# Two more gate blocks as a pair by seven products, and the constants of linear attention built earlier

## The chip, the cores and the metric

The kernel runs on one core of a Trainium2 chip. The metric is the device time in microseconds of one launch, from the first instruction to the last; a profile of one execution gives the time of every instruction on each engine: TensorE (PE, with its weight loads PEld), VectorE (DVE), ScalarE (ACT), GpSimd (POOL), and SyncE (SP), whose queue issues most transfers (DMA).

## What is computed

One layer of a streaming encoder over T = 1056 tokens (1024 of a prompt, 32 of a sample), width 1024:

```python
h = rms(x); z = h @ w_in   # GLA q,k,v,r,rank | band q,k,v | merge gates ga, gb
oa, s_gla = gla_branch(qa, ka, va, ra, alr, ...)      # 4 heads, causal gated linear recurrence
ob, k_rows, v_rows = attn_fn(qb, kb, vb, rel_bias)     # 8 heads, 64-frame chunks, band of 8 chunks back
mix = (sigmoid(ga) * (oa @ w_br_a) + sigmoid(gb) * (ob @ w_br_b)) @ w_out
x = x + rms_norm(mix, g_post_mix)
f, conv_new = conv_ffn(rms_norm(x, g_pre_ffn), conv_s0, w_up, conv_w, conv_b, w_down)
x = x + rms_norm(f, g_post_ffn)
x = x + rms_norm(sigmoid(rms_norm(x, g_pre_ple) @ w_ple_gate) * (pe @ w_ple), g_post_ple)
```

The gates `ga` and `gb` are 1024 columns of `w_in` each, so 8 blocks of 128 columns each. The outputs are y for both groups, the newest band rows, the states of linear attention (`o_gp` of the prompt, `o_gs` of the sample) and of the convolution.

## The kernel before

Tokens lie along the free axis, features on the 128 partitions. Every large product is made of three matmuls in fp32r: a value is split into a high part and the rest (`whi`, `wlo` of weights, `xh`, `xl` of the input), and high x high, high x low and low x high are summed in PSUM. A high part is made by ACT, a low part by DVE or POOL. One block of 128 weight columns over all tokens (`project`) is 8 feature tiles x 3 spans of 352 tokens x 3 = 72 matmuls of 352 columns; a third of it, one span, is 24.

The program runs: the norm of x (its sums `accx` and the result `rstd` are DVE's), four pairs of band heads (`band_project`, scores `s`, sums `sm`), four heads of linear attention (GLA), the gates, the merge, `w_out`, and the ConvFFN, whose large products `two` take seven products of half blocks.

A GLA head (`gla_head`) takes 8 chunks of 128 prompt tokens and the sample as the ninth. Per chunk PE transposes (`kt`), makes scores level by level, DVE copies them under the `masks` (`copy_predicated`), and PE multiplies scores by `vt` (L977) and state by queries (L979); DVE updates `state` (L989, three buffers). The sample's state is loaded into such a buffer (L970). `out_o_gp` and `out_o_gs` are stored by SP when the last states are there. A norm of the outputs `ot` follows (ACT square L997, DVE L999, split L259 and L260, matmuls L262 and L263, ACT, DVE). The masks (7 levels), `eye` and zeroed score tiles are built once by `constants`, with 28 affine selects on POOL and 8 casts on DVE, when GLA starts.

Gate blocks are made in two ways. Plain: `gates` calls `project`. By seven products: `gate_pair` takes two blocks of weights and halves of tokens and features and makes seven products of 4 feature tiles x 2 spans of 264 tokens x 3 = 24 matmuls each (`b11`, `b21`, `b22`, `t4`, `t2`, `t1`, `t3`), 168 in all. Three of them, and `t4` over the input's own quarter, need sums of quarters of x: these are made in the band (`quarter_sums`, tiles `tt`), stored to `d_t` in DRAM, and loaded again in eight transfers (`quarter_load`, L1039) and split (L1043 on ACT, L1044 on DVE) when `take` asks for them. Before the change the blocks 2 to 7 of `ga` are plain; the other two of `ga` and the eight of `gb` make five pairs.

Program order is not issue order: a scheduler sorts the instructions of every engine by data, buffers and priority, and the plain gates, written after the last head, fill PE between that head's small matmuls. Each engine and each queue then runs its rows strictly in that order. Pools bound what can move: `gp` (GLA's tiles) has to be released before `tp` and `gs` (tiles of the pairs) can be allocated, and `sums_left` (transfers that add up quarters of `w_down`) is drained first. `third_sum` (L1612) forms one input of the ConvFFN's `t3` by a subtraction of 128 x 1056 on POOL, twice.

Of the kernel before, what the change touches and what calls it, by code (L numbers as in the profile page):

```python
# [12 lines left out]
F32R = mybir.dt.float32r  # L13
# [4 lines left out]
P = 128  # L18
# [44 lines left out]
PLAIN_GATES = (2, 3, 4, 5, 6, 7)  # L63
# [58 lines left out]
def emit(tc, a):  # L122
# [365 lines left out]

    d_ob = tl(dram, [4, P, T], tag="d_ob")
# [198 lines left out]
    def quarter_sums(k):  # L688
        a1, a2, b1, b2 = [[t[:, r].bitcast(F32) for t in (xh, xl)] for r in (k, k + HK) for _ in range(2)]
        n = HT // QN  # L690
        for j in range(QN):
            p, q = slice(j * n, (j + 1) * n), slice(HT + j * n, HT + (j + 1) * n)
            A, S = ALU.add, ALU.subtract
            t = tl(bp, [P, n], tag="tt", bufs=12)
# [4 lines left out]
            t = tl(bp, [P, n], tag="tt", bufs=12)  # L699
# [4 lines left out]
            u = tl(bp, [P, n], tag="tt", bufs=12)  # L704
# [3 lines left out]
            t = tl(bp, [P, n], tag="tt", bufs=12)  # L708
# [4 lines left out]
    for hp in range(4):  # L713
# [34 lines left out]
        if hp:  # L748
            band_norm(hp - 1)
    bp.release()  # L750
# [15 lines left out]
    masks, eye, scores, scores_s = None, None, [], None  # L766


    def constants():
        nonlocal masks, eye, scores_s  # L770
        masks = tl(gp, [P, 7, P], U8, tag="masks")
        scores.extend(tl(gp, [P, 2 * P], tag=f"scores{i}") for i in range(2))
        for l in range(7):
            m = 1 << l
            mf = scores[l % 2][:, :P]
            po.memset(mf, 1.0)
            for j in range(2):
                v = blocks(mf, m)[:, :, m * j : m * j + m]
                first = m * (1 - j)
                pat = [[-2 * m, 64 // m], [0, m]]  # L780
                po.affine_select(out=v, in_=v, pattern=pat, compare_op=ALU.is_ge, fill=0.0, base=-first, channel_multiplier=1)
                pat = [[2 * m, 64 // m], [0, m]]
                po.affine_select(out=v, in_=v, pattern=pat, compare_op=ALU.is_ge, fill=0.0, base=first + m - 1, channel_multiplier=-1)
            ve.tensor_copy(masks[:, l], mf)
        eye = tl(gp, [P, P], U8, tag="eye")
        ve.tensor_copy(eye, ident)
        for i in range(2):
            po.memset(scores[i], 0.0)
        scores_s = tl(gp, [NS, NS], tag="scores_s")
        po.memset(scores_s, 0.0)  # L790

    DG = (192, 0)
    TOGETHER = ((4,3,2,1),(6,5))
    SEGS = [(0, 256), (256, 256), (512, 256), (768, 288)]

    def blocks(t, m):
        return t.rearrange("p (n s) -> p n s", s=2 * m)

    def apart(t, m):
        return bass.AP(t.tensor, t.offset, [t.ap[0], [2 * m, 64 // m], [P + m, 2], [1, m]])  # L800

# [1775 lines left out]
```

## Time and profile before

| | |
|---|---|
| median of 3 runs | 1895.81 us (1894.96 to 1901.61) |
| profiled execution | 1895.03 us, its span 1893.3 us |
| PE busy | 1866.0 us, 99% |
| DVE busy | 1347.5 us, 71% |
| ACT busy | 905.2 us, 48% |
| POOL busy | 434.0 us, 23% |

The span runs from the first to the last instruction of the profiled execution; busy times are those of instructions that compute, and matmuls that overlap count once. All stretches and start times below are microseconds from the span's start.

### The profile page before, as it was taken

What the parts mean: (1) busy time and instruction counts of PE and PEld (TensorE: products, weight loads), DVE (VectorE), ACT (ScalarE), POOL (GpSimd) and SP (SyncE); (2) the same over time, 40 slices, a digit from 0 to 9 for tenths busy, and PEclk for the clock granted to TensorE, in tenths of its full rate; (3) what the DMA queues carried; (4) which work ended last, traced back from release to release, by engine and by line L of the source; (5) the groups of instructions that cost most, each with busy time, mean ns of one, the idle gap of its engine ahead of it and who ended that gap; (6) DMA issues with size and microseconds to landing.
All of it is one profiled execution on the core that took longest, in us unless ns stands there. A gap on an engine that the chain in (4) does not pass through costs nothing.

```text
span 1893.3 us, 34755 instructions
## 1 busy us (share of the span) xinstructions
PE 1866.0 (99%) x13484; PEld 1836.2 (97%) x13484; DVE 1347.5 (71%) x2713; ACT 905.2 (48%) x1709; POOL 434.0 (23%) x548
## 2 busy tenths in 40 slices
PE   9999999999999999999999999999999999999997
PEld 8999999989999999999999999999999999999997
DVE  6657577678787774887463887987777776556886
ACT  7455465445454564544234564433333345445554
POOL 2312232342212121003210212332222222115312
PEclk9999999999999999999999999999999999999999
DMA  7324356452423433695484446543433448656677
GB/s 277 122 98 151 114 156 161 136 147 68 111 68 109 124 114 112 232 356 218 123 333 146 145 152 225 189 167 127 149 133 121 148 161 293 193 182 205 209 265 149
DMA packets 112417, 316.46 MB, mean 167 GB/s; under 512 B 14004, under 2 KB 39036, under 8 KB 112124
## 3 DMA queue, kind: packets, MB, share of 16 engines
q1 hardware_dynamic: 86124, 226.30, 35.5%
q0 software_dynamic: 25296, 87.04, 15.9%
q8 instruction: 106, 1.74, 0.4%
q10 hardware_dynamic: 832, 0.90, 0.1%
q14 instruction: 59, 0.48, 0.1%
HBM read 222.12 MB, written 111.93 MB: 176 GB/s over the span
## 4 chain that ended last, share of the span: by engine, by line
PE 84%; DVE 7%; issue 3%; ACT 3%; DMA 1%; POOL 0%; SPq 0%; ACTq 0%; DVEq 0%; POOLq 0%
PE mm L240 12%; PE mm L241 12%; PE mm L242 12%; PE c L2003 11%; PE two L1739 6%; PE two L1741 6%; PE two L1740 6%; PE aux L2003 2%; PE mm L1089 2%; PE mm L1091 2%; PE mm L1090 2%; PE one L615 2%; PE one L573 2%; PE two L919 1%; PE two L557 1%
## 5 line engine op out<-in xcount | busy, mean ns | idle before, releaser
L240 PE MATMUL mm<-xh,whi 128*128 128x352 f32 (+2 forms) x1008 | 333.5, 331 | 1.7 <-DVE q L813 1.1
L242 PE MATMUL mm<-xh,wlo 128*128 128x352 f32 (+2 forms) x1008 | 331.5, 329 | 0.0
L241 PE MATMUL mm<-xl,whi 128*128 128x352 f32 (+2 forms) x1008 | 330.3, 328 | 0.0
L220 POOL TENSOR_TENSOR wlo<-raw,whi 128x512 fp32r<-128x512 f32 x108 | 155.9, 1450 | 657.6 <-ACT whi L219 628.0
L240 PEld LDWEIGHTS mm<-xh,whi 128*128 128x128 f32 x1008 | 190.1, 189 | 3.9 <-DVE q L813 1.4
L242 PEld LDWEIGHTS mm<-xh,wlo 128*128 128x128 f32 x1008 | 189.4, 188 | 1.9 <-issue 1.0
L241 PEld LDWEIGHTS mm<-xl,whi 128*128 128x128 f32 x1008 | 189.9, 188 | 1.0
L1741 PE MATMUL two<-mh,wlo 128*128 128x264 f32 x576 | 162.9, 284 | 0.0
L1740 PE MATMUL two<-ml,whi 128*128 128x264 f32 x576 | 162.5, 283 | 0.0
L1739 PE MATMUL two<-mh,whi 128*128 128x264 f32 x576 | 161.3, 284 | 0.4 <-ACT whi L245 0.4
L219 ACT ACTIVATE whi<-raw 128x512 fp32r<-128x512 f32 x116 | 72.5, 628 | 119.4 <-PE mm L241 72.3
L2003 PE MATMUL c<-mh,whi 128*128 128x264 f32 x396 | 112.4, 284 | 0.0
L2003 PE MATMUL c<-mh,wlo 128*128 128x264 f32 x396 | 112.2, 283 | 0.0
L2003 PE MATMUL c<-ml,whi 128*128 128x264 f32 x396 | 112.2, 283 | 0.0
L1740 PEld LDWEIGHTS two<-ml,whi 128*128 128x128 f32 x576 | 108.3, 188 | 0.0
L1741 PEld LDWEIGHTS two<-mh,wlo 128*128 128x128 f32 x576 | 108.3, 188 | 0.0
L1739 PEld LDWEIGHTS two<-mh,whi 128*128 128x128 f32 x576 | 107.3, 188 | 0.6 <-ACT whi L245 0.6
L1729 ACT ACTIVATE whi<-ws 128x512 fp32r<-128x512 f32 x72 | 45.3, 629 | 89.0 <-PE two L1740 52.2
L566 ACT ACTIVATE s<-s,sm 128x640 f32<-128x640 f32 (+5 forms) x72 | 50.3, 698 | 58.5 <-DVE sm L564 57.2
L240 PE MATMUL mm<-mh,ahi 128*128 128x352 f32 x240 | 77.4, 322 | 0.0
L241 PE MATMUL mm<-ml,ahi 128*128 128x352 f32 x240 | 77.4, 322 | 0.0
L242 PE MATMUL mm<-mh,alo 128*128 128x352 f32 x240 | 77.3, 322 | 0.0
(649 smaller groups left out, 5929.1 us busy)
## 6 DMA issues: line engine op xcount, KB each, us to landing
raw<-in_w_in SPq DMA_DIRECT2D x51, 512.0 KB, 3.9
uraw<-d_b POOLq DMA_DIRECT2D x33, 528.0 KB, 4.9
raw<-in_w_up SPq DMA_DIRECT2D x26, 512.0 KB, 3.7
d_b<-av POOLq DMA_DIRECT2D x44, 264.0 KB, 2.7
d_s<-in_w_down POOLq DMA_DIRECT2D x16, 704.0 KB, 8.0
draw<-d_s SPq DMA_DIRECT2D x16, 704.0 KB, 4.2
hn<-d_b POOLq DMA_DIRECT2D x40, 264.0 KB, 3.8
d_b<-hn POOLq DMA_DIRECT2D x40, 264.0 KB, 2.5
```

Source lines behind the costliest of these rows:

```text
L219: ac.activation(hi[-1][:, d], raw[:, b], AF.Copy)
L220: eng.tensor_tensor(lo[-1][:, d], raw[:, b], hi[-1][:, d], op=ALU.subtract)
L240: pe.matmul(ps, h, xh(kt), start=(first and i == 0), stop=False)
L241: pe.matmul(ps, h, xl(kt), start=False, stop=False)
L242: pe.matmul(ps, l, xh(kt), start=False, stop=(last and i == n - 1))
L566: ac.activation(s, s, AF.Exp, scale=-1.0, bias=sm[:nq], accum_out=sums[:nq, q0 // P : q0 // P + 1])
L573: pe.transpose(tp[:n, i * nq : (i + 1) * nq], s[:, k0 : k0 + n], ident[:nq, :nq])
L1729: ac.activation(h, x, AF.Copy)
L1739: pe.matmul(ps[:, j, :HC], w[0][:, k], x[0][:, k, s], start=st, stop=False, skip_group_check=True)
L1740: pe.matmul(ps[:, j, :HC], w[0][:, k], x[1][:, k, s], start=False, stop=False, skip_group_check=True)
L1741: pe.matmul(ps[:, j, :HC], w[1][:, k], x[0][:, k, s], start=False, stop=sp_, skip_group_check=True)
L2003: pe.matmul(ps, w, x, start=st, stop=sp_, skip_group_check=True)
```

## The change

- Blocks 2 and 3 of `ga` leave the plain gates and become a sixth pair by seven products.
- The first two products of the first pair, `b11` and now `b21` (it was `b22`), are written ahead of the drain of `sums_left`, of the release of `gp` and of the pools `tp` and `gs`. What the first `take` calls loaded and split in steps over three products is asked for at the third.
- `constants` moves from GLA's start into the band loop, at the second pair of band heads with low priority, with a pool `cp` of its own that is released with `gp`.
- `tt` has 8 buffers in place of 12, and `third_sum` runs on DVE.

```diff
-PLAIN_GATES = (2, 3, 4, 5, 6, 7)
+BEFORE = 2
+PLAIN_GATES = (4, 5, 6, 7)
...
+    cp = pool("cp")
...
-            t = tl(bp, [P, n], tag="tt", bufs=12)
+            t = tl(bp, [P, n], tag="tt", bufs=8)
...
+        if hp == 1:
+            with low(QLOW):
+                constants()
...
-    constants()
     got = gla_project(0)
...
     gates(len(PLAIN_GATES))
-    for _ in sums_left:
-        pass
-    gp.release()
...
             (lambda: weight("b11", a11), m_b11),
+            (lambda: weight("b21", a12), m_b21),
             (for_b22, m_b22),
-            (lambda: weight("b21", a12), m_b21),
...
-    todo = [(w + n, lambda i, g, d=d, n=n: gate_done(d, n + i, g)) for w, d, ns in ((GB0, d_gb, (0, 2, 4, 6)), (GA0, d_ga, (0,))) for n in ns]
+    todo = [(w + n, lambda i, g, d=d, n=n: gate_done(d, n + i, g)) for w, d, ns in ((GB0, d_gb, (0, 2, 4, 6)), (GA0, d_ga, (0, 2))) for n in ns]
...
+    unit(0)[0]()
+    unit(1)[0]()
+    for i in range(BEFORE):
+        unit(i + LOOK)[0]()
+        unit(i)[1]()
+    for _ in sums_left:
+        pass
+    gp.release()
+    cp.release()
...
-    unit(0)[0]()
-    unit(1)[0]()
-    for i in range(7 * len(todo)):
+    for i in range(BEFORE, 7 * len(todo)):
         if unit(i + LOOK):
             unit(i + LOOK)[0]()
-        take(FIRST_SUMS[i] if i < 7 else 0)
+        take(sum(FIRST_SUMS[:i + 1]) if i == BEFORE else FIRST_SUMS[i] if i < 7 else 0)
...
     def third_sum(j):
-        po.tensor_tensor(XS["b22", j], XS["b22", j], XS["b12", j], op=ALU.subtract)
+        ve.tensor_tensor(XS["b22", j], XS["b22", j], XS["b12", j], op=ALU.subtract)
```

What the scheduler makes of it is seen in the order of each engine. PE, the sample's part of the last head, before (L977 and L979 are the sample's outputs from scores and state, L950 its state's update, `mm` a plain gate):

```order
L241 MATMUL mm_8758<-xl_134,whi_8698 128x352
L950 MATMUL one_8186<-vt_7230,kt_8188 128x256
L242 MATMUL mm_8758<-xh_133,wlo_8699 128x352
L240 MATMUL mm_8758<-xh_133,whi_8702 128x352
L241 MATMUL mm_8758<-xl_134,whi_8702 128x352
L242 MATMUL mm_8758<-xh_133,wlo_8703 128x352
L977 MATMUL one_8203<-scores_s_4292,vt_7230 128x32
L979 MATMUL one_8203<-x_8085,state_8201 128x32
L977 MATMUL one_8203<-scores_s_4292,vt_7230 128x32
L979 MATMUL one_8203<-x_8085,state_8201 128x32
L240 MATMUL mm_8758<-xh_133,whi_8702 128x352
L241 MATMUL mm_8758<-xl_134,whi_8702 128x352
```

and in the changed kernel, where L983, L985 and L956 are the same three, L263 and L264 the matmuls of the norm, and L1066 and L1067 the first pair's `b22`:

```order
L953 MATMUL one_8189<-ident_79,x_8088 32x128
L983 MATMUL one_8206<-scores_s_2413,vt_7233 128x32
L985 MATMUL one_8206<-x_8088,state_8204 128x32
L983 MATMUL one_8206<-scores_s_2413,vt_7233 128x32
L985 MATMUL one_8206<-x_8088,state_8204 128x32
L956 MATMUL one_8189<-vt_7233,kt_8191 128x256
L263 MATMUL one_8218<-y_1444_8219,onesHr_77 128x288
L264 MATMUL one_8218<-y_1445_8220,onesHr_77 128x288
L1066 MATMUL mm_8820<-xh_133,whi_8715 128x264
L1067 MATMUL mm_8820<-xl_134,whi_8715 128x264
```

The rows of gate matmuls between them are gone: the plain gates that are left, and b11 and b21, stand earlier, and b22 stands behind the norm's matmuls.

SP's queue, from the first loads of `d_t` to the stores of the last states, before:

```order
L1039 DMA ev_8917<-d_t_553 128x2x528
L1039 DMA ev_8958<-d_t_553 128x2x528
L1039 DMA ev_8996<-d_t_553 128x2x528
L672 DMA d_ga_548<-fe_8603 128x1056
L1062 DMA raw_9111<-in_w_in 128x1024
L1005 DMA d_oa_4236<-ot_8021 128x2x256
L992 DMA out_o_gp<-state_8183 128x256
L970 DMA state_8201<-in_state_gla 128x256
L994 DMA out_o_gs<-state_8209 128x256
```

and in the changed kernel:

```order
L976 DMA state_8204<-in_state_gla 128x256
L998 DMA out_o_gp<-state_8186 128x256
L1000 DMA out_o_gs<-state_8212 128x256
L1177 DMA ev_8802<-d_t_556 128x2x528
L1177 DMA ev_8808<-d_t_556 128x2x528
L1177 DMA ev_8814<-d_t_556 128x2x528
L1177 DMA ev_8853<-d_t_556 128x2x528
L1011 DMA d_oa_4290<-ot_8143 128x2x288
L1177 DMA ev_8891<-d_t_556 128x2x528
L1177 DMA ev_8897<-d_t_556 128x2x528
```

All loads of `d_t` (L1177 now) have moved behind `out_o_gs`; of before, three stand ahead of it.

DVE, the last sum of the first norm and the norm of the next span, before:

```order
L362 TENSOR_TENSOR accx_135<-accx_135,xin_132 128x704
L406 TENSOR_TENSOR ev_430<-mm_467,ev_430 16x352
L271 TENSOR_TENSOR y_88_516<-y_87_515 128x352
L272 SCALAR_TENSOR_TENSOR y_88_516<-y_88_516,one_513 128x352
L273 SCALAR_TENSOR_TENSOR rstd_84<-y_88_516,y_87_515 128x352
```

and in the changed kernel, where L508 is the cast of a finished mask:

```order
L363 TENSOR_TENSOR accx_135<-accx_135,xin_132 128x704
L407 TENSOR_TENSOR ev_430<-mm_467,ev_430 16x352
L508 CAST masks_2364<-scores_454_2365 128x128
L508 CAST masks_2364<-scores_455_2366 128x128
L508 CAST masks_2364<-scores_454_2365 128x128
L508 CAST masks_2364<-scores_455_2366 128x128
L272 TENSOR_TENSOR y_88_516<-y_87_515 128x352
L273 SCALAR_TENSOR_TENSOR y_88_516<-y_88_516,one_513 128x352
L508 CAST masks_2364<-scores_454_2365 128x128
L274 SCALAR_TENSOR_TENSOR rstd_84<-y_88_516,y_87_515 128x352
```

Five of the eight casts stand here, four ahead of the norm and one inside it. On POOL the selects that they wait for stand directly behind `MEMSET ev 80x1056` (L480 before), the last third of them around the next two `wlo`.

## Rows read from the trace of the kernel before

**Rows 1.** The page, part 1: busy time of each engine and share.
```profile
PE 1866.0 (99%) x13484; PEld 1836.2 (97%) x13484; DVE 1347.5 (71%) x2713; ACT 905.2 (48%) x1709; POOL 434.0 (23%) x548
```

**Rows 2.** The page, part 4: the chain that ended last, by engine.
```profile
PE 84%; DVE 7%; issue 3%; ACT 3%; DMA 1%; POOL 0%; SPq 0%; ACTq 0%; DVEq 0%; POOLq 0%
```

**Rows 3.** Waits of PE over the whole span: total us, times, longest us.
```profile
PE two L557 <- DVE sm L564: 2.3, 4, 1.6
PE two L1653 <- DVE wlo L1639: 2.0, 2, 1.8
...
PE one L955 <- ACT kt L937: 1.2, 1, 1.2
...
PE one L977 <- DVE sct L967: 0.2, 1, 0.2
```

**Rows 4.** Stretches: length, busy us and count by engine, clock, DMA share, GB/s.
```profile
704.82:708.71 3.89, 3.89 (x25) 3.89 (x25) 3.89 (x18) 2.97 (x11) 0.00 (x0) 1.00 0.49 162
760.48:862.61 102.13, 102.13 (x842) 102.13 (x841) 85.71 (x154) 53.15 (x94) 4.02 (x3) 1.00 0.85 303
702.00:864.00 162.00, 162.00 (x1226) 160.05 (x1225) 121.21 (x250) 85.05 (x149) 10.45 (x8) 1.00 0.66 236
```

**Rows 5.** Timeline of POOL and DVE, 1164 to 1177 us: start, duration, operation.
```profile
1164.41 2.58 POOL L1612 TENSOR_TENSOR hn<-hn,hx 128x1056 f32<-128x1056 f32 x1 [3.95 <-DMA hn<-d_hn]
...
1164.95 3.12 DVE L1518 TENSOR_TENSOR av<-gc,av 128x1024 f32<-128x1024 f32 x1 [0.30 <-ACT gc L1517]
...
1171.37 3.05 DVE L1512 SCALAR_TENSOR_TENSOR gc<-gx,vec,gc 128x1058 f32<-128x1058 f32 x1 [0.48 <-ACT gc L1511]
...
1176.30 1.25 DVE L1592 TENSOR_TENSOR t3l<-hn,t3h 128x1056 fp32r<-128x1056 f32 x1
```

**Rows 6.** Line 1518, all its runs: ns min/median/max, first and last start.
```profile
L1518 DVE TENSOR_TENSOR av<-gc,av x22: 1216/1219/3123, 1165.0 to 1572.3; 128x1024 f32<-128x1024 f32 x22
```

**Rows 7.** Timeline of ACT and DVE in the last head's tail.
```profile
740.69 0.99 DVE L967 COPY_PREDICATED scores_s<-masks,one 32x16 f32<-32x16 uint8 x5
...
747.45 0.69 ACT L997 ACTIVATE sq<-ot 128x576 f32<-128x576 f32 x1
...
748.16 0.46 DVE L999 SCALAR_TENSOR_TENSOR sq<-sq 128x288 f32<-128x288 f32 x1 [2.04 <-ACT sq L997]
...
749.15 0.43 ACT L259 ACTIVATE y<-sq 128x288 fp32r<-128x288 f32 x1
...
749.89 0.45 DVE L260 TENSOR_TENSOR y<-sq,y 128x288 fp32r<-128x288 f32 x1
```

**Rows 8.** Landings of the loads of lines 970 and 1039; splits, lines 1043, 1044.
```profile
DMA to landing us min/median/max: 2.1/2.5/2.8
...
DMA to landing us min/median/max: 3.5/3.9/4.2
...
L1043 ACT ACTIVATE xh<-ev x4: 626/631/649, 757.3 to 759.4; 128x528 fp32r<-128x528 f32 x4
...
L1044 DVE TENSOR_TENSOR t2l<-ev,t2h x4: 701/702/704, 766.8 to 769.0; 128x528 fp32r<-128x528 f32 x4
```

**Rows 9.** Timeline of SP's queue: the first loads of `d_t`.
```profile
719.38 2.01 SPq L1039 DMA_DIRECT2D ev<-d_t  x3
```

**Rows 10.** Timeline of POOL and DVE at the start of the band.
```profile
51.30 1.28 POOL L220 TENSOR_TENSOR wlo<-raw,whi 128x512 fp32r<-128x512 f32 x1 [15.12 <-ACT whi L219]
...
53.63 0.52 DVE L271 TENSOR_TENSOR y<-y 128x352 f32<-128x352 f32 x1 [5.01 <-ACT y L270]
...
54.74 1.47 DVE L273 SCALAR_TENSOR_TENSOR rstd<-y,y 128x352 f32<-128x352 f32 x1
```

**Rows 11.** Groups of POOL, 376 to 391 us: busy us, mean ns.
```profile
L783 POOL TENSOR_SCALAR_AFFINE_SELECT scores<-scores 128x64 f32<-128x64 f32 x14 | 5.3, 500 | 0.0
L781 POOL TENSOR_SCALAR_AFFINE_SELECT scores<-scores 128x64 f32<-128x64 f32 x14 | 5.1, 508 | 0.1
```

**Rows 12.** Line 640, all its runs: ns min/median/max, first and last start.
```profile
L640 DVE TENSOR_TENSOR ev<-ot x8: 172/186/193, 121.1 to 380.1; 64x32 f32<-64x32 f32 x8
```

More of the change, by code (lines that the diff above doesn't have):

```diff
@@ L486, in emit, with constants, blocks, apart @@
     ap.release()
+    cp = pool("cp")
+    masks, eye, scores, scores_s = None, None, [], None
+    def constants():
+        nonlocal masks, eye, scores_s
+        masks = tl(cp, [P, 7, P], U8, tag="masks")
+        scores.extend(tl(cp, [P, 2 * P], tag=f"scores{i}") for i in range(2))
+        for l in range(7):
+            m = 1 << l
+            mf = scores[l % 2][:, :P]
+            po.memset(mf, 1.0)
+            for j in range(2):
+                v = blocks(mf, m)[:, :, m * j : m * j + m]
+                first = m * (1 - j)
+                pat = [[-2 * m, 64 // m], [0, m]]
+                po.affine_select(out=v, in_=v, pattern=pat, compare_op=ALU.is_ge, fill=0.0, base=-first, channel_multiplier=1)
+                pat = [[2 * m, 64 // m], [0, m]]
+                po.affine_select(out=v, in_=v, pattern=pat, compare_op=ALU.is_ge, fill=0.0, base=first + m - 1, channel_multiplier=-1)
+            ve.tensor_copy(masks[:, l], mf)
+        eye = tl(cp, [P, P], U8, tag="eye")
+        ve.tensor_copy(eye, ident)
+        for i in range(2):
+            po.memset(scores[i], 0.0)
+        scores_s = tl(cp, [NS, NS], tag="scores_s")
+        po.memset(scores_s, 0.0)
+    DG = (192, 0)
+    TOGETHER = ((4,3,2,1),(6,5))
+    SEGS = [(0, 256), (256, 256), (512, 256), (768, 288)]
+    def blocks(t, m):
+        return t.rearrange("p (n s) -> p n s", s=2 * m)
+    def apart(t, m):
+        return bass.AP(t.tensor, t.offset, [t.ap[0], [2 * m, 64 // m], [P + m, 2], [1, m]])
     d_ob = tl(dram, [4, P, T], tag="d_ob")
@@ L703, in quarter_sums @@
             dma.dma_start(d_t[2, k][:, p], t)
-            u = tl(bp, [P, n], tag="tt", bufs=12)
+            u = tl(bp, [P, n], tag="tt", bufs=8)
             ve.tensor_tensor(u, t, a1[0][:, p], op=A)
@@ L764, in emit @@
     wa2 = None
[L766 to L800, printed above, removed]
     def gla_project(h):
@@ L1019, in emit @@
     gates(len(PLAIN_GATES))
-    for _ in sums_left:
-        pass
-    gp.release()
     one, two = slice(0, HT), slice(HT, T)
-    tp = pool("tp")
-    XS = {n: [tl(tp, [P, HK, HT], F32R, tag=n + x) for x in "hl"] for n in ("t1", "t2", "t3")}
+    XS = {}
     XS["b11"] = [t[:, 0:HK, one] for t in (xh, xl)]
@@ L1030, in emit @@
     XS["t4"] = [t[:, 0:HK, two] for t in (xh, xl)]
[L1031 to L1032 removed]
+    gs = None
     def slot():
         return tl(gs, [P, T], tag="slot", bufs=SLOTS)
[L1037 to L1057 removed]
     def gate_pair(n1, n2, done, fresh):
```

45 lines of the change are left out of this document (24 added, 21 removed).

## The prediction

> **What bounds the kernel now.** I read the busy times first, then the chain of work that ended last, then the waits of TensorE (PE), then single stretches. PE is busy 1866.0 of 1893.3 us [rows 1]: the whole span holds some 27 us without a matmul in it, and the start and end of the program are in that. The chain is 84% PE, DVE has 7% [rows 2]. So an edit pays either by taking matmul time away or by closing one of PE's few waits, and it loses by opening a new one; work on DVE, ACT, POOL or the queues counts only through such a wait. The waits that this change can reach are four [rows 3]: 2.3 us on `sm` (1.6 of it at the band's start), 2.0 us on `wlo` L1639, 1.2 us on `kt` L937 and 0.2 us on `sct` L967, the last two in the last head of linear attention (at 696.13 and 701.32). From 702 to 864 us PE is busy 162.00 of 162.00 us [rows 4], and that is where most of the change happens: there is nothing to gain there but matmul time, and much to lose.
>
> **The change, part by part.**
>
> *The sixth pair.* Two plain gates are 144 matmuls of 352 columns, the pair by seven products is 168 of 264. A third of a plain gate, 24 matmuls, takes 3.89 us; the five pairs, 840 matmuls, take 102.13 us, PE busy throughout [rows 4]. Two gates are 6 x 3.89 = 23.3 us, a pair is 102.13/5 = 20.4 us: **-2.9 us**. The sums and splits that a pair brings lie in a stretch where DVE is busy 85.71 of 102.13 us and PE never waits [rows 4], so they cost nothing; without that cover a DVE operation of some 0.7 us would show now and then. I keep -2.6 as the poor end.
>
> *`third_sum` on DVE.* On POOL the first takes 2.58 us, to 1166.99. The DVE operation L1518 that begins meanwhile takes 3.12 us, to 1168.07 [rows 5], where 22 runs of it have a median of 1.219 us [rows 6]: it did next to nothing until POOL was done. L1512, which meets the second sum, takes 3.05 us [rows 5]. So POOL now costs DVE about 1.9 + 1.8 = 3.7 us, and on DVE the two sums would cost 2 x 1.25, by `t3l` of the same size [rows 5]. DVE comes out 1.2 us ahead, and what waits for it is PE's 2.0 us on `wlo` [rows 3]. I take **-1.2 us**; bounds 0 (the transfer of `hn` ends later than DVE) and -2.0 (all of that wait).
> The Trainium skill, "SBUF — State Buffer", Who interferes with whom, says the same of a DVE instruction with two inputs in SBUF and a GpSimd one that reads SBUF: one fully blocks the other. By that rule the constants, which this change puts beside such DVE work, are the danger; see the third rival.
>
> *The last head's early part.* 23 instead of 14 gate matmuls now stand between the transposes and the first one that waits for `kt`, and 12 more behind it. The two waits of 1.2 and 0.2 us [rows 3] go: **-1.4 us** (poor end -0.7).
>
> *The head's tail without fill.* Before, plain gates stand between the last chunk's small matmuls. Now they are used up when the tail comes: 18 rows of PE follow one another, and b22, the third product, stands behind L264. Three waits come in the open. The masked copies into `scores_s` take 0.99 us [rows 7] and a first short one behind the L962 matmuls (L968 now); some four matmuls on PE cover about half of that: 0.55. The sample's state lands 2.1 to 2.8 us after its issue [rows 8], which itself has to wait until PE has read a state buffer; I count 0.55 left over, by hand. The norm of the sample chunk is ACT 0.69, DVE 0.46, ACT 0.43, DVE 0.45 [rows 7], 2.03 us in a row and by my estimate 2.45 with the eviction ahead of it and the hops between engines; in its place PE has one matmul of a third of a microsecond, so 2.1. Together **+3.2 us**; 2.0 if only the norm shows, 5.0 if the state's whole load does.
>
> *The loads of `d_t`.* Before, the first three are issued from 719.38 on, within 2.01 us [rows 9], some 40 us ahead of the pairs at 760.48. Now the release holds all eight behind `out_o_gs` in SP's queue, and that waits for DVE's update of the sample's state, the last thing of the tail. By my hand chain that is near 743.1 on the old clock of the trace; a load lands 3.5 to 4.2 us later [rows 8], and several in one go land some 1.4 to 1.8 us apart (my estimate: 528 KB each at the 303 GB/s that the pairs' stretch moves [rows 4], or somewhat more). The first is there near 746.8, its half-sums `xh` and `xl` 0.63 and 0.70 us later each [rows 8]. b22's 24 matmuls (2.9 us) begin near 744.4 and end near 747.4. So t4 waits for about 0.7. On DVE two evacuations of t4 stand ahead of the four `t2l`, which then take 4 x 0.70: t2 ends about 1.7 later than its matmuls need. Ahead of t1 and t3 stand matmuls of the second pair, 24 each, which I take as cover. **+2.4 us**; bounds 0 (loads and splits all inside b22) and +6.0 (landings as late as the raw weights behind one another in the same queue, and t3's first half late too).
>
> *The constants in the band.* The 28 selects take 5.3 + 5.1 us [rows 11], with the memsets some 12. POOL sits idle for 15.1 us before 51.30 us, DVE for 5.0 us before 53.63 [rows 10]; both hold the work, if the casts and selects take their turns. What is behind is the norm whose last step, L273, stretched to 1.47 us at 54.74 [rows 10], and DVE is then nearly full until PE's 1.6 us on `sm` [rows 3]. One cast of 0.2 lies right ahead of L273. **+0.4 us**; bounds 0 and +3. Taking them out of 376 to 391 us gives nothing that I can show: POOL's next `wlo` waits for ACT there.
>
> *The rest*: four `tt` buffers fewer (each is used again 8 tiles later, and its store has landed by then), the accumulating transfer ahead of its place, the order of b21 and b22: no wait of PE near any of them, 0.
>
> **The sum.** -2.9 - 1.2 - 1.4 + 3.2 + 2.4 + 0.4 = +0.5 us. The profiled execution took 1895.03 us (its span 1893.3 and 1.7 around it), 0.8 below the median of the three runs, so 1895.5 there and **1896.2 us** by the median. I take 0.5% (9.5 us) as what a measurement can tell from no change: 1886.3 and 1905.3.
>
> **The rivals.**
>
> *1. The tail is hidden.* The two products ahead of the release and the second pair's weights fill the waits, and only the norm shows: -2.9 - 1.2 - 1.4 + 2.0 + 0.4 + 0 = -3.1, so **1892.7 us**, and with the whole `wlo` wait gone 1891.9. For it: DVE and ACT are not half busy there, and the hand chain counts every hop. Against it: the PE rows show no fill at all in the tail, an engine takes its rows in order, and a load of 3.5 us is longer than b22's 2.9 us.
>
> *2. Slower: the loads set the end.* One mechanism: eight loads behind `out_o_gs`, the fifth to eighth each waiting for a buffer that a split has to free, the raw weights between them. If t3's first half lands only when the second pair's b11 is done, PE waits for t4, t2 and t3 in turn, +6.0 instead of +2.4: **1899.8 us**; and 1901.6 if the whole load of the state shows too. It decides from landings of 4.5 us upward (b22 plus the norm's end). To pass +0.5% it would need 15 us of waits in place of 5.6. For it: nothing stands behind b22 that doesn't need `d_t`. Against it: 3.5 to 4.2 in all eight cases now.
>
> *3. The selects and DVE shut each other out at 36 to 48 us.* DVE's sums there have two inputs in SBUF, as in [rows 5]. With 10.4 us of selects [rows 11], most of them in turn with DVE's work, and 5.0 us idle to take it up [rows 10], the norm comes some 3 us later (10.4 less 5.0, less the 2 us or so of selects that fall beside DVE's casts and waits), and hardly anything behind it is free: +3.0 instead of +0.4, **1898.8 us**. By the skill's rule this would be so. Against it: `ev<-ot` L640, two inputs in SBUF, last runs at 380.1 us, among the selects, and none of its eight runs is over 193 ns [rows 12]; one short instruction is thin evidence.
>
> *4. The change doesn't do what it says*: the sixth pair runs no faster than two plain gates since the stretch is short of DMA or DVE. PE is busy 102.13 of 102.13 us in five of them [rows 4], so I give it no chance of its own.
>
> **How the numbers follow.** The forecast (within 2 us of 1896.2) 0.48; the first rival 0.24; the second 0.16; the third 0.12. The range, 1891 to 1901, takes in the first rival with its best ends and nearly all of the second; what is left out is under 0.2, mostly waits that I haven't seen. The likeliest case alone spans 1894 to 1898.5. Faster by over 0.5% would take 9.5 us, more than all the gains together: 0.02. Slower by over 0.5% needs the second and third together or something unseen: 0.04. The rest, 0.94, is within 0.5%.
>
> **What would show it.** Right: five or six waits of PE of 0.3 to 2.2 us between about 735 and 765, led by the norm's `y` (L263/L264) and by `xl` or `t2l`; none at the old 696.13 and 701.32; L1512 and L1518 at 1.2 to 1.3 us around 1165 to 1175 and the wait on `wlo` down to about 0.8; each of the six pairs 20.4 us. Wrong: no wait at L264 or at t4 (rival 1); t3 waiting over 1 us with loads landing over 4.5 us after issue (rival 2); DVE's sums at 36 to 48 us over 1 us each and the wait on `sm` over 3 us (rival 3). A wait of PE that doesn't exist now, outside 36 to 80, 690 to 780 and 1160 to 1185, would mean that I missed an effect.

## The result, and the profile after

The changed kernel takes **1906.68 us** (median of 6 runs, 1904.56 to 1910.26) beside 1897.22 us for the kernel before in the same comparison (6 runs, 1894.96 to 1901.61): a ratio of **1.005, 95% interval 1.004 to 1.006**. The forecast was 1896.2 us, its range 1891 to 1901. The change is slower by 9.5 us, which is outside the range and about the 0.5% that the prediction took as what a measurement can tell from no change.

The profiled execution of the changed kernel took 1907.11 us. First its page, part 1, as in [rows 1]:
```profile
span 1905.3 us, 34826 instructions
...
PE 1872.2 (98%) x13508; PEld 1841.8 (97%) x13508; DVE 1356.5 (71%) x2736; ACT 901.7 (47%) x1712; POOL 426.9 (22%) x542
```
The span is 12.0 us longer than before, and this line splits it: PE is *busy* 6.2 us longer, although the change takes matmul time away, and what is left without a matmul grows from 27.3 to 33.1 us, by 5.8.

Next the waits of PE in the changed kernel, in the columns of [rows 3]:
```profile
PE mm L241 <- DVE slot L1073: 2.7, 1, 2.7
PE two L594 <- DVE sm L601: 2.7, 5, 1.8
PE one L264 <- DVE y L261: 2.0, 1, 2.0
...
PE one L263 <- ACT y L260: 1.4, 1, 1.4
...
PE mm L1067 <- DVE t2l L1182: 1.0, 1, 1.0
PE mm L1066 <- ACT t1h L1181: 0.7, 1, 0.7
...
PE one L983 <- ACT ot L987: 0.6, 1, 0.6
```
The 1.8 us on `wlo` and those on `kt` and `sct` are gone. The five lines below `sm`, and the first one, do not exist before. The first and third of the list are the ones that the prediction had not seen.

Then stretches of the changed kernel, in the columns of [rows 4]; the third column from the end is the granted clock:
```profile
60.00:80.00 20.00, 18.22 (x104) 17.92 (x103) 15.95 (x28) 11.36 (x20) 10.23 (x10) 0.91 0.65 203
680.00:700.00 20.00, 18.04 (x110) 17.83 (x109) 12.89 (x46) 10.43 (x25) 4.84 (x3) 0.91 0.52 140
740.00:760.00 20.00, 16.99 (x110) 15.44 (x109) 14.06 (x35) 10.03 (x21) 0.00 (x0) 0.83 0.58 180
768.86:871.11 102.25, 102.25 (x842) 102.18 (x841) 85.42 (x155) 46.35 (x84) 4.02 (x3) 1.00 0.76 276
860.00:880.00 20.00, 17.30 (x123) 17.04 (x122) 17.24 (x30) 12.84 (x28) 6.12 (x4) 0.93 0.84 327
```
The fourth line is five pairs, 102.25 us where [rows 4] has 102.13: the pair saves its 2.9 us. In the other four the mean clock is below 1.00. In the profiled execution of the kernel before it is 1.00 in all of these places (it is lower, 0.76, only in the last stretch of the program):
```profile
60.00:80.00 20.00, 18.38 (x116) 18.07 (x116) 16.38 (x30) 11.92 (x22) 11.32 (x10) 1.00 0.64 198
680.00:700.00 20.00, 18.79 (x122) 18.40 (x121) 12.60 (x42) 12.47 (x28) 7.41 (x5) 1.00 0.45 115
740.00:760.00 20.00, 20.00 (x124) 18.94 (x122) 9.86 (x24) 10.48 (x17) 0.00 (x0) 1.00 0.16 57
860.00:880.00 20.00, 20.00 (x131) 20.00 (x131) 16.37 (x26) 11.44 (x25) 7.61 (x5) 1.00 0.92 350
```
In each of the four places of the changed kernel the clock is at its lower level, 1.2 of 2.4 GHz, for some 3 to 7 us. In three of them it falls within 1.5 us of the end of a wait of PE (1.78, 1.96 and 2.70 us); in the fourth it falls at 747.7, as the wait of 1.42 us begins and not behind it. PE's 1866.0 us less 2.9 should have been 1863.1; it is 1872.2, and the **9.1 us** between are what half clock adds to the matmuls (by the granted clock of these four stretches and of 880 to 900, 0.98, it is 8.8 us). That and the new waits make up the 12.0 us between the two profiles: -2.9 + 9.1 + 5.8.

The two profiles lie further apart than the medians (12.0 and 9.5 us), because the profiled execution of the kernel before lost less clock than most: of its 70 executions beside the experiments the 18 with a mean clock of 0.998, like the profiled one, have a median of 1894.8 us, the 35 at 0.996 have 1897.2, and the ten at 0.995 have 1898.8. So some 2 us of half clock belong to the kernel before as well, and by that estimate the change adds nearer 7 us of it than 9.1.

Two of the new waits, each at its place. VectorE near 695 us, and the wait of PE behind it, start and duration:
```profile
690.26 0.42 DVE L904 TENSOR_TENSOR x<-x,k 128x256 f32<-128x256 f32 x1
694.15 0.69 DVE L1047 TENSOR_TENSOR early<-early,raw 128x512 f32<-128x512 f32 x1 [3.46 <-DMA raw<-in_w_in]
...
695.73 0.42 DVE L261 TENSOR_TENSOR y<-sq,y 128x256 fp32r<-128x256 f32 x1
```
```profile
696.20 0.39 PE L264 MATMUL one<-y,onesHr 128*128 128x256 f32 x1 [1.96 <-DVE y L261]
```
A sum of weights for the first pair (L1047, in `for_b22`) stands on VectorE ahead of the last head's `y`. Its weights had been asked for at 689.42, and VectorE stood for 3.46 us with `y` behind it; PE waits 1.96 us at L264. Before, these sums came at 723 us, where PE waited for nothing. VectorE and PE near 875 us:
```profile
873.65 2.11 DVE L1073 TENSOR_TENSOR slot<-slot,mm 128x264 f32<-128x264 f32 x6
```
```profile
875.91 0.40 PE L241 MATMUL mm<-bh,whi 128*128 128x352 f32 x1 [2.70 <-DVE slot L1073]
```
The second span of the b-product takes a PSUM bank. By the program's allotment, which no profile prints, that is in the changed kernel bank 7, which holds the last pair's `Y1`, the last thing that VectorE empties; in the kernel before the last pair's `Y` lies in banks 2 and 3 and the b-product begins in 4 and 7. One pair more turns the allotment on.

And the loads of `d_t`, as in [rows 8] (four are issued from 748.67 on, two from 757.05, two from 759.91; seven have a landing in the trace):
```profile
DMA to landing us min/median/max: 5.0/6.3/7.9
```

### The profile page after: what moved, and what is told of

It reads as the page before. It is cut to its first block, busy times and chain, and to the rows that moved or that the text cites. A ratio compares the mean times of both kernels' runs of the same rounds, so it can differ in the third digit from the quotient of the medians.

```text
span 1905.3 us, 34826 instructions
## 1 busy us (share of the span) xinstructions
PE 1872.2 (98%) x13508; PEld 1841.8 (97%) x13508; DVE 1356.5 (71%) x2736; ACT 901.7 (47%) x1712; POOL 426.9 (22%) x542
## 4 chain that ended last, share of the span: by engine, by line
PE 55%; DVE 5%; ACT 2%; DMA 1%; issue 1%; SPq 0%; DVEq 0%; ACTq 0%
PE c L2016 11%; PE two L1752 6%; PE two L1754 6%; PE two L1753 6%; PE mm L242 5%; PE mm L241 5%; PE mm L243 5%; PE aux L2016 2%; PE mm L1066 2%; PE mm L1068 2%; PE mm L1067 2%; DVE z L2122 1%; DMA ev<-d_t 1%; DVE acc L2079 0%; DMA gc<-d_hn 0%
## 5 line engine op out<-in xcount | busy, mean ns | idle before, releaser
L241 PE MATMUL mm<-xh,whi 128*128 128x352 f32 (+2 forms) x960 | 319.1, 332 | 1.8 <-DVE q L819 1.1
L243 PE MATMUL mm<-xh,wlo 128*128 128x352 f32 (+2 forms) x960 | 317.0, 330 | 0.0
L242 PE MATMUL mm<-xl,whi 128*128 128x352 f32 (+2 forms) x960 | 316.0, 329 | 0.0
L221 POOL TENSOR_TENSOR wlo<-raw,whi 128x512 fp32r<-128x512 f32 x104 | 150.8, 1456 | 671.8 <-ACT whi L220 655.5
L241 PEld LDWEIGHTS mm<-xh,whi 128*128 128x128 f32 x960 | 182.1, 190 | 4.3 <-DVE q L819 1.4
L243 PEld LDWEIGHTS mm<-xh,wlo 128*128 128x128 f32 x960 | 181.5, 189 | 1.4 <-issue 0.7
L242 PEld LDWEIGHTS mm<-xl,whi 128*128 128x128 f32 x960 | 181.8, 189 | 1.0
```

Of the source, the lines that this page charges most:

```text
L221: eng.tensor_tensor(lo[-1][:, d], raw[:, b], hi[-1][:, d], op=ALU.subtract)
L241: pe.matmul(ps, h, xh(kt), start=(first and i == 0), stop=False)
L242: pe.matmul(ps, h, xl(kt), start=False, stop=False)
L243: pe.matmul(ps, l, xh(kt), start=False, stop=(last and i == n - 1))
```

## The experiments

Times are medians of 4 to 19 executions (g1: one), ratios those to the kernel before, run beside each; "rest" is the span of the profiled execution less PE's busy time.

| run | us | ratio (95%) | span | PE busy | rest |
|---|---|---|---|---|---|
| before | 1895.5 to 1897.6 | 1 | 1893.3 | 1866.0 | 27.3 |
| changed | 1906.68 | 1.005 (1.004, 1.006) | 1905.3 | 1872.2 | 33.1 |
| g1 changed again | 1906.57 | | 1904.9 | 1871.7 | 33.2 |
| e1 sum on VectorE | 1894.79 | 0.9984 (0.9975, 0.9993) | 1891.7 | 1865.9 | 25.8 |
| i1 rest of change | 1897.14 | 1.0007 (0.9997, 1.0017) | 1895.2 | 1869.0 | 26.2 |
| f1 five pairs | 1902.89 | 1.0031 (1.002, 1.0043) | 1901.3 | 1872.3 | 29.0 |
| e5 other banks | 1901.62 | 1.0022 (1.0013, 1.0032) | 1899.6 | 1870.2 | 29.4 |
| h2 before, bad bank | 1902.14 | 1.0026 (1.0014, 1.0037) | 1899.8 | 1870.6 | 29.2 |
| e2 constants late | 1906.07 | 1.0044 (1.0027, 1.0061) | 1903.4 | 1872.0 | 31.4 |
| e4 sums moved | 1906.26 | 1.0043 (1.0028, 1.0058) | 1904.8 | 1872.3 | 32.5 |
| f2 none ahead | 1913.44 | 1.009 (1.0061, 1.012) | 1910.5 | 1875.5 | 35.0 |
| h3 loads elsewhere | 1904.49 | 1.0041 (1.0025, 1.0056) | 1902.5 | 1869.5 | 33.0 |
| f4 tail fill | 1907.22 | 1.0053 (1.0032, 1.0074) | 1904.1 | 1869.1 | 35.0 |
| f3 b21 in the tail | 1901.79 | 1.0036 (1.0023, 1.0049) | 1898.7 | 1867.1 | 31.6 |
| h1 busy at 876 | 1909.28 | 1.0059 (1.0043, 1.0074) | 1908.8 | 1875.2 | 33.6 |
| k1 busy tail | 1905.45 | 1.0055 (1.0042, 1.0067) | 1901.9 | 1873.5 | 28.4 |
| m1 wide busy tail | 1907.85 | 1.0062 (1.0045, 1.0078) | 1906.8 | 1874.6 | 32.2 |

**e1: `third_sum` alone, on the kernel before.**
```
-        po.tensor_tensor(XS["b22", j], ...)
+        ve.tensor_tensor(XS["b22", j], ...)
```


> The kernel before with one edit: the two third_sum operations of the b-product on VectorE in place of GpSimd. Theory A (the sum on GpSimd and VectorE's own sums hold one another up, and VectorE is what PE waits for at wlo): PE's wait of 1.83 us at 1176 us goes, the VectorE operations L1512 and L1518 there fall from 3.1 to 1.2 us, and the time is 1.9 us lower, about 1895.3 beside 1897.2. Theory B (PE waits for a transfer there, so the engine of the sums does not matter): the wait stays within 0.3 us of 1.83, and the time stays within 0.5 us.

All 22 runs of the operation of [rows 6], in this run:
```profile
L1518 DVE TENSOR_TENSOR av<-gc,av x22: 1217/1220/1225, 1166.3 to 1571.4; 128x1024 f32<-128x1024 f32 x22
```
The one of 3.12 us is gone, and the wait of 1.83 us with it (0.93 on `whi`, ScalarE's, stays in its place). Theory A: 2.4 us by the medians, 1.6 by the spans of the two profiles. The gain of 0.16% (0.07 to 0.25) makes this **the fastest of all kernels here**, faster than before and than the change.

**e5 and h2: the bank, taken away and put in.** e5 is the changed kernel with the wide PSUM laid out so that, by the program's allotment, its first spans get banks 1, 4, 3 and 2; h2 is the kernel before with its first spans on 0 and 3.
```
e5:  -    banks[:] = [MODE, 8 - MODE, 0]
     -    ps_one()
     +    banks[:] = [MODE, 7 - MODE, 0]
     +    tl(psum, [P, 512], tag="pad", bufs=1)
     +    ps_mm()
h2:  -    ps_one()
     +    ps_mm()
```


> The changed kernel with one edit: the PSUM banks behind the pairs are laid out so that no product of the first span of the b-product takes the bank that holds the last pair's Y1 (one buffer fewer for single tiles). Theory A (the wait of 2.70 us at 875.9 us is a bank that VectorE has yet to empty, and the half clock behind it costs 1.7 us): no wait of over 0.7 us from 860 to 880 us, clock 1.00 from 860 to 900 us, and the time 4.0 to 4.5 us below the changed kernel. Theory B (VectorE is late there whatever the bank, its L246 slowed by GpSimd's wlo): the wait only moves to the next operation that needs VectorE, 2 us or more of it within 20 us, and the time falls by under 1 us.

> The kernel before with one edit: the four banks of the matmul tiles behind the pairs are 0 to 3 in place of 4 to 7, so that the b-product's second span takes the bank of the last pair's Y1, as in the changed kernel. Theory A (the bank alone makes the wait at 876 us): a wait of 2.0 to 2.9 us on slot by VectorE near 868 us, and the time 2.5 to 4.5 us above the kernel before. Theory B (the sixth pair makes VectorE late there, and the bank only shows it): a wait below 0.7 us, and the time within 1 us.

The stretch of e5, a wait of PE in h2, and two stretches of h2:
```profile
860.00:880.00 20.00, 20.00 (x148) 20.00 (x146) 17.42 (x31) 12.62 (x27) 6.12 (x4) 1.00 0.86 333
```
```profile
PE mm L240 <- DVE slot L1096: 2.7, 1, 2.7
```
```profile
380.00:400.00 20.00, 18.99 (x100) 17.71 (x99) 6.04 (x19) 4.88 (x12) 11.10 (x35) 0.79 0.50 129
860.00:880.00 20.00, 17.29 (x121) 17.02 (x121) 16.05 (x29) 11.51 (x25) 6.50 (x5) 1.00 1.00 395
```
Without the bank PE does not wait there; with it the kernel before waits as the changed one does. Theory A, twice, and half of the slowdown. The times move by more than the wait, and a little more than theory A said: -5.1 us (1906.68 to 1901.62) and +4.6 (1897.57 to 1902.14). In the changed kernel there was half clock behind the wait (0.93 above), which e5 lacks. In h2 (and in e2 below) the clock stays at 1.00 behind the same wait; it falls near 380, ahead of anything that h2 edits, so what the time of h2 moved beyond the 2.7 us is not explained.

**f1 and i1: the sixth pair undone, then also the products ahead of the release.** f1 sets `PLAIN_GATES` to (2, ..., 7) and gives the first factor one pair by seven products; i1 also has `BEFORE = 0`, b22 ahead of b21 again, and first spans on banks 3, 6 and 5.

> The changed kernel with the sixth pair undone: gates 2 and 3 of the first factor are plain again, two products still stand ahead of the release, the rest of the change stays. Theory A (what costs is that the sixth pair takes 144 matmuls of fill out of the last head and shifts the PSUM banks): PE's order up to the pairs is that of the kernel before, the waits at 696, 745 to 763 and 876 us are gone, the waits on kt and sct (1.2 and 0.2 us) are back, and the time is within 1.5 us of the kernel before with third_sum on VectorE, 1893.5 to 1896.5. Theory B (the release behind two products, the constants or the later loads of d_t cost): at least half of the 9.5 us between the two kernels stays, 1901 us or more.

> What is left of the change without the sixth pair and without products ahead of the release: five pairs in the old order of their products (b22 second), third_sum on VectorE, the constants in the band, the new place of the pools, four tt buffers fewer; the wide PSUM laid out so that the first three spans of the b-product meet no bank of the last pair's Y. Theory A (these parts cost nothing that can be measured): no wait from 700 to 880 us over 0.7 us, and the time within 1.2 us of the kernel before with third_sum on VectorE, 1893.6 to 1896.0. Theory B (the constants in the band or the pools carry part of the slowdown): 1897 us or more, with a wait at 74 us of over 1.75 us or a new one.

f1 is not what theory A said, and 1902.89 is past B's bound. The waits at 696, 745 and 876 are gone as A had it, but three others are there, 3.9 us from 768 to 778. ScalarE, and PE behind it, in f1:
```profile
764.25 1.28 ACT L706 ACT_TABLE_LOAD   x1
765.55 1.09 ACT L706 ACTIVATE fe<-fe 128x1056 f32<-128x1056 f32 x1
766.65 1.28 ACT L251 ACT_TABLE_LOAD   x1
767.95 0.39 ACT L1076 ACTIVATE early<-mm 128x264 f32<-128x264 f32 x1
```
```profile
768.39 0.39 PE L1066 MATMUL mm<-xh,whi 128*128 128x264 f32 x1 [2.09 <-ACT early L1076]
```
With b21 right behind b11 in one accumulation, PE needs b11's copy before it can go on, and that copy stands behind the last gate's sigmoid and two table loads. So the products ahead of the release have a cost of their own. i1, without them, has there only 0.56 and 0.28 us of waits on `t2l` and `t1h` at 778, and its 1897.14 us can't be told from the kernel before. It misses A's bound by 1.1 us and meets both marks of B (1.79 us at 74): against before it stands 3.1 us behind e1 by the medians, 4.4 by the ratios. In the profiles, 3.5 us apart, the clock makes most of it: PE is busy 3.1 us longer in i1, which has half clock between 380 and 400, where the clock of e1 is 1.00:
```profile
380.00:400.00 20.00, 18.36 (x98) 17.30 (x98) 5.44 (x13) 6.21 (x13) 2.56 (x2) 0.84 0.40 116
```
h2, which has none of these parts, has it there too, so it isn't shown to be their doing.

**f2: no product ahead of the release, six pairs** (`BEFORE = 0`).

> The changed kernel with no product ahead of the release (BEFORE 0 in place of 2); the sixth pair stays. Theory A (the two products are the only fill that the last head's end has): no first-pair product stands among the last chunk's small matmuls, PE waits there for scores, kt and sct too, 2 to 4 us more than the changed kernel between 735 and 755 us, while the wait on t2l goes (1.0 us); the last pair's banks also fall otherwise, so that the wait at 876 us goes; together 1902 to 1906 us. Theory B (the two products are nothing that PE lacks): waits between 735 and 765 us as in the changed kernel, within 0.5 us.

A wait of PE and a stretch in f2:
```profile
PE one L961 <- ACT kt L943: 3.3, 1, 3.3
...
740.00:760.00 20.00, 18.18 (x99) 16.26 (x100) 12.57 (x31) 8.43 (x19) 0.00 (x0) 0.69 0.58 204
```
Theory A as to the place (PE waits 3.25 us on `kt` where the changed kernel doesn't), and worse than its numbers, 1913.4: PE was at half clock for most of 738 to 756, and the wait at 880 did not go (2.02 us). The two products are the tail's fill; two plain gates were more of it.

**e2 and e4: the constants put back behind the band; the first pair's sums behind the norm.**
```
e2:  -        if hp == 1:
     -            with low(QLOW):
     -                constants()
     +    constants()
          got = gla_project(0)
e4:  +            with tc.issue_after(first_normed[0]) if fresh and len(sums) > 1 else ...:
                      ve.tensor_tensor(t, x, y, op=o)
```


> The changed kernel with one edit: the constants of linear attention are built after the band again, in the same pool as in the change. Theory A (the constants cost by the late norm on VectorE, 0.15 us of wait, and by the half clock that follows the longer wait at 74 us, 1.5 us): the wait on sm is 1.6 us again, the granted clock is 1.00 from 60 to 80 us, and the time is 1.6 to 2.1 us below the changed kernel. Theory B (the clock falls after that wait by itself and its length does not matter): the wait is shorter, the clock from 60 to 80 us stays near 0.91, and the time falls by 0.2 us at most.

> The changed kernel with one edit: the sums of weights for the first pair stand on VectorE behind the first segment's norm of the last head, not ahead of its y. Theory A (the wait of 1.96 us at 696.2 us is the y behind a sum that waits 3.5 us for its weights, and the half clock after it costs 1.7 us more): that wait goes, the clock from 680 to 700 us is 1.00, the small waits on kt and sct that stood there in the kernel before (1.2 and 0.2 us) may come back, and the time is 2.2 to 3.7 us below the changed kernel. Theory B (only waits count, the clock's fall is not their doing): the wait goes, the clock there stays near 0.91, and the time falls by 0.5 to 2.0 us.

e2 moves hardly anything (0.6 us less by the medians): the wait on `sm` is 1.75 us, as in the second profile of the changed kernel (g1), so the constants are not what lengthens it. Its clock, in two stretches:
```profile
60.00:80.00 20.00, 18.25 (x114) 17.95 (x113) 17.09 (x31) 11.88 (x22) 10.72 (x10) 1.00 0.66 209
...
380.00:400.00 20.00, 19.05 (x103) 17.97 (x102) 4.56 (x11) 4.51 (x10) 2.57 (x2) 0.78 0.32 96
```
That wait leaves the clock at 1.00 here, and it falls at 378 instead, where the changed kernel had 1.00. Neither theory. In e4 the wait on `y` is gone and the clock from 680 to 700 is 1.00, as its theory A had it, but `kt` (0.77 and 0.60) and `sct` (1.07) take the wait's place, 2.4 us for 1.96, half clock comes near 380 instead (0.78), and the time stays, which neither theory said. The head has too little fill, whichever of its operations waits.

**h3: the loads of `d_t` by GpSimd's queue**, on e5 (`po.dma_start` for `dma.dma_start` in `quarter_load`).

> The changed kernel with the banks of the earlier run, and the eight loads of d_t issued by GpSimd's queue in place of SP's, so that they do not stand behind out_o_gs. Theory A (the loads are late because SP is held by the store that waits for VectorE): they are issued more than 5 us earlier, the waits on t2l and t1h (1.0 us, in some executions 0.7 more) go, and the time is 1.0 to 3.0 us below the 1901.6 of the banks alone. Theory B (buffers of the pool ev or the splits' tiles behind the release hold them back, or GpSimd's queue is itself busy): issued within 2 us of before, the waits stay within 0.4 us, and the time within 0.7 us.

The first three are issued at 704 in place of 748, and the wait on `t2l` goes: SP's order did hold them. The time rises by 2.9 us all the same. VectorE in h3, and waits of PE:
```profile
715.26 0.53 DVE L474 TENSOR_TENSOR fe<-mm,rstd 128x352 f32<-128x352 f32 x1 [6.47 <-DMA d_ga<-fe]
```
```profile
PE one L263 <- ACT y L260: 4.9, 2, 2.9
```
The gates have one buffer `fe`, which is free when its store has landed. Beside the three loads that store took 8.6 us from issue to landing, 3.5 in e5; VectorE stood 6.47 us for it, 1.36 in e5, and behind it were the inputs of the head's next norm: PE waits 2.92 us there. A as to the cause, wrong as to the time.

**g1: the changed kernel once more; h1, k1, m1, f4, f3: what brings half clock.** g1 has no edit. h1 is the changed kernel with 20 useless matmuls of 264 columns in the wait at 876, into a PSUM bank that is taken from the others for it. k1 and m1 are e5 with useless matmuls in the tail, behind the sample's products and ahead of its norm: 24 of 128 columns, 13 of 248. f4 and f3 put the second half of b21, 12 matmuls of 264, there; f4 also lowered the priority of the 288-column norms of all heads.
```
h1:  +            if n == 0 and c == 1:
     +                for i in range(IDLE):
     +                    pe.matmul(idle, hi[0][:, i % 4], bh[:, i % 4, :HC], ...)
k1:  +                with tc.high_priority(), tc.issue_after(tail[0]):
     +                    for i in range(IDLE):
     +                        pe.matmul(full[1][:, 384:], w[n][0][:, 0], x[0][:, i % 4, :P], ...)
f3:  +                with tc.issue_after(tail[0]) if fresh and n == "b21" and j else ...:
```


> The changed kernel once more, unedited, for a second profile. Theory A (which of the longer waits is followed by half clock differs from execution to execution; each time costs 1.5 to 2 us): the same waits within 0.3 us, the clock below 1.00 at other places than 60 to 80, 680 to 700, 740 to 760 and 860 to 900 us in at least one case. Theory B (the clock falls behind every wait above some length): the same places.

> The changed kernel with 20 matmuls of 264 columns more that nothing uses, into a PSUM bank of their own, right ahead of the second span of the b-product, where PE waits 2.70 us for the last pair's Y1. They fill 2.4 us of the wait and take nothing off it. Theory A (the wait is paid twice, by itself and by the half clock behind it): PE's idle time at 876 us is below 0.5 us, the clock from 860 to 900 us is 1.00, the end of the second span's wait stays where it is, and the time is 1.2 to 2.0 us below the changed kernel's 1906.7, although PE does more. Theory B (the half clock comes from something else in this stretch, such as load on the memory or VectorE, or it costs nothing): clock below 1.00 there as before, time within 0.5 us of 1906.7 or above.

> The changed kernel with the banks of the earlier run and 24 matmuls of 128 columns more that nothing uses, into the unused columns of a PSUM bank, between the last chunk's small matmuls and its norm, where PE waits 1.42 us and ran at half clock behind it in every profile so far with the banks and the changed kernel. Theory A (half clock follows from PE standing still there): the idle time at L264 falls below 0.3 us, the clock from 740 to 760 us rises from 0.91 to 0.97 or more, b22's matmuls behind it come every 0.12 us from the first on, and the time is 0.8 to 2.0 us below the 1901.6 of the banks alone. Theory B (the small matmuls of the tail are what lowers the clock, busy or not): the clock there stays at 0.91 or below and the time within 0.5 us.

> As the run before with useless matmuls in the last head's tail, at the same place in PE's order, but 13 of 248 columns in place of 24 of 128. Theory A (what the engine streams in the tail decides: the small matmuls of 32 to 128 columns count for little, wide ones hold the clock): the clock from 740 to 760 us is 0.97 or more, b22's matmuls come every 0.12 us, and the time is 1 to 3 us below the 1905.5 of the run with 128 columns. Theory B (the tail falls to half clock whatever stands at that place): the clock there is 0.83 to 0.91 as in the earlier runs, and the time within 1 us of that run.

> The changed kernel with the banks of the earlier run and with the second half of the first pair's b21 product (12 matmuls, 1.5 us) queued on PE behind the last chunk's products, ahead of its norm. Theory A (the 1.42 us on the norm is a wait without fill): the wait on y at L263 is below 0.3 us, the chain of small matmuls starts earlier and its own waits (0.58 us) grow by at most 1 us, and the time is 1 to 3 us below the run with the banks alone, 1898.5 to 1900.5. Theory B (the tail is a chain through VectorE, ScalarE and PE that sets its own length): what the norm's wait loses comes back on scores, sct and scores_s, and the time stays within 0.7 us of 1901.6.

> The changed kernel with the banks of the earlier run, and with the second half of the first pair's b21 product (12 matmuls of 264 columns) behind the last chunk's products and ahead of its norm, with the priority of all norms left alone (in the earlier run of this idea it was lowered for all heads, which opened waits elsewhere). Theory A (useful wide matmuls in the tail hold the clock there, and the rest of the tail's length is set by its own chain): the clock from 740 to 760 us is 1.00, the waits there sum to 3 to 4.5 us, and the time is 0 to 2 us below the 1901.6 of the banks alone. Theory B (the order in the tail does not matter): the clock there is 0.91 or below and the time within 0.7 us of 1901.6.

g1 has the longer waits of the first profile, 1.75 us at 694.93 among them, but 1.00 from 680 to 700: with nearly the same wait the clock once fell and once didn't. Neither theory as written: one of the four places is missing and none is new. In h1 the wait is 0.23 us and the clock beside it full:
```profile
860.00:880.00 20.00, 19.77 (x149) 19.58 (x149) 16.89 (x30) 12.62 (x27) 6.12 (x4) 1.00 0.88 343
880.00:900.00 20.00, 20.00 (x125) 20.00 (x125) 12.35 (x23) 8.34 (x19) 5.59 (x4) 1.00 0.38 119
```
From that point to L1757 at 1193.65 h1 takes 318.6 us, the changed kernel 319.9: 1.3 us better with as many useful matmuls. But its whole time is not better (1909.28); waits of 1.08 us at 1232 and of 1.31 and 0.87 at 1595, where the changed kernel has only one of 0.61, came with the edit. So A holds at the place, and the total neither shows it nor the contrary.

k1 settles something else. PE in k1 around the fill, and the stretch:
```profile
746.83 0.69 PE L959 MATMUL one<-vt,kt 32*128 32x256 f32 x2
747.45 3.88 PE L1078 MATMUL mm<-xh,whi 128*128 128x128 f32 x24
751.12 0.55 PE L264 MATMUL one<-y,onesHr 128*128 128x288 f32 x1
751.47 0.44 PE L265 MATMUL one<-y,onesHr 128*128 128x288 f32 x1
751.71 0.42 PE L1070 MATMUL mm<-xh,whi 128*128 128x264 f32 x1
```
```profile
740.00:760.00 20.00, 19.03 (x126) 17.79 (x125) 12.43 (x31) 7.82 (x17) 0.00 (x0) 0.83 0.47 161
```
There is no wait at L264 any more, and the clock falls at 749.4 all the same and stays down to 756 (in e5 from 750 to 753.5). So standing still at the norm is not needed for it. What stands ahead of the fall is a wait of 0.58 us at 745 and, from 742 on, only small matmuls, of 16 to 256 columns, where the kernel before has those of plain gates between them; which of these counts was not tested apart. With wide matmuls at the same place (m1) the clock falls at 750 too, as they begin, and is back at 753.4. f4 kept 1.00 through the whole tail; f3, with the same idea, fell from 743 to 747. So the clock goes by the B of k1, m1 and f3, the time by it in f3 alone (k1 is 3.8 us above e5, m1 2.4 above k1), and f4 meets neither of its theories: only half an answer. None of the five beats e5: what one wait in the tail loses the next one gains (f3: 0.28, 0.72, 1.11, 1.23, 0.99; e5: 0.28, 0.58, 1.42, 0.99), and the edits open waits elsewhere (f4: 2.19 us at 667, on the sample's state).

## Why the prediction was wrong

**The step that failed is the sum itself**: it took matmul time at the clock of [rows 4], 1.00 in each stretch, as fixed, set every wait at its own length, and in the head's early part counted PE's matmuls alone. Three terms are not in it: the half clock (9.1 us of PE's time between the two profiles, nearer 7 by the estimate above, and still the largest), the PSUM bank (2.7 us) and `y` behind VectorE's sums of weights (1.96 us). The mechanisms in order:

- *The sixth pair*, -2.9: right (102.25 us for five).
- *`third_sum`*, -1.2: right in kind, and a little small. The wait of 1.83 us goes, one of 0.93 on `whi` stays, and e1 is 2.4 us faster by the medians (1.3 to 4.7 by the interval), 1.6 in the profiles. The Trainium skill, "SBUF — State Buffer", Who interferes with whom, gives this lock between a VectorE operation with two inputs in SBUF and GpSimd's reads, and e1's row agrees (3.12 us to 1.22).
- *The last head's early part*, -1.4: `kt` and `sct` went, but 1.96 us on `y` came in their place. I had counted the matmuls on PE and not what the same move puts into VectorE's queue.
- *The tail without fill*, +3.2: 2.0 measured. The norm's wait is there, 1.42 for 2.1. At the first matmul on `scores_s` it is 0.58 for 0.55, but that is in part luck: the profile lets it end with ScalarE's `ot` (L987, done at 745.53), the copies that the term was made of were done at 745.26. The state's load showed nothing.
- *The loads of `d_t`*, +2.4: 1.0 and 0.7 us. The landings, 5.0 to 7.9 us, are above the 4.5 from which the second rival decides, but its wait on `t3` over 1 us came only in g1 (1.03). The 3.5 to 4.2 us that the prediction went by are the landings of two loads, not of eight: the other six, three of them issued within 2 us, have none in the trace of before. t4's part, 0.7, does not show because half clock slowed b22: where b22 ran at full clock, PE waits 1.23 (f3) and 1.24 us (f4) for `xl`.
- *The constants*, +0.4: 0.2, and e2 says that not even this is theirs. The third rival's cost did not come. VectorE's sums in the changed kernel, most of them beside the selects, mean ns last before the idle time:
```profile
L363 DVE TENSOR_TENSOR accx<-accx,xin 128x704 f32<-128x704 f32 x6 | 5.4, 894 | 0.3
```
They took 890 ns in the kernel before. So the rule of that section of the Trainium skill, that the two shut each other out, does not show on VectorE's side here. The selects themselves took 6.2 + 6.0 us where [rows 11] has 5.3 + 5.1; whether VectorE held them up was not tested.
- *Not in the sum*: 2.7 us for a PSUM bank. The prediction named a wait outside its places as the sign of an effect missed, and this is one. (The sum itself, +0.5 on the median of 1895.81, gives 1896.3, not 1896.2; it changes nothing.)

**Where the 9.5 us lie**, by the ratios to before: -0.16% with `third_sum` alone; +0.07% with all but the sixth pair and its early products (i1); +0.22% with those as well and good banks (e5); +0.50% with the bank (the change). The step from i1 to e5 has -2.9 us of matmuls in it, so what comes with the sixth pair and its early products in the last head costs more than the pair brings. Of this the bank is shown by taking it away and putting it in, and the fill of the tail by f2; how the rest divides among `y`, the loads and the clock is argued from the profiles.

**What stays open**: why the clock falls in one place and not in another. Behind `sm` at 74 us, with 1.6 to 1.8 us of wait, it fell in three of seventeen profiles (changed, g1, h3); around 378, with 1.45 us, in ten, and never in those three. The Trainium skill, "TensorE: Matmul & The Clock Gate", What's actually happening, says that throttled is the default and activity releases it, on a clockwork that runs on whatever the kernel does; the spread agrees, but no run here sets that clockwork. The price was not isolated by an edit over a whole execution either (h1); what there is are the executions of the kernel before, 4.0 us apart between mean clocks of 0.998 and 0.995.

## What to carry to other kernels

Matmuls that look like plain throughput may be the fill that keeps PE busy through a chain of small operations: before a faster form replaces them, count the chain's waits without them, and add to the sum what half clock may cost: in this case it was of the size of the waits themselves (9.1 us and 5.8 in one profile), though it didn't come behind every wait. A change in the number of PSUM tiles turns the allotment for everything behind it: look at which bank the next stage's first products take and who empties it last. And where a step moves ahead on one engine, list what it puts into the queues of the others.

## What was not expected of the hardware

Two executions of one program, with the same waits, have their half clock at different places (changed and g1), and h2, which is edited behind the pairs only, has one near 378 where the profiled execution of the kernel before has none. Behind a wait of 2.7 us for the same bank the clock fell in the changed kernel and stayed at 1.00 in h2 and e2. Matmuls of 128 columns one behind the other did not hold the clock (k1). Loads of 528 KB that landed in 3.5 and 4.2 us one by one took 5.0 to 6.8 us when four were issued within 2 us, and 5.6 to 7.9 us in twos with loads of weights between them.
